# One encoder layer on one core: head groups moved in single transfers, high parts on the lower rows

## The chip, the cores and the metric

The kernel runs on one core of one Trainium2 chip. The number that counts is device time in microseconds (us) of one execution, start to end. Engines have the names of the profile: PE is the matrix engine (TensorE), PEld its weight loads, DVE is VectorE, ACT is ScalarE, POOL is GpSimd, SP is SyncE, which only issues transfers here. A transfer (DMA) issued by SP is carried out by 16 DMA engines that serve the core.

## The reference

One layer of a transformer encoder over x, 2048 tokens of 1024 floats, all in float32. Two groups of 8 query heads (head size 64, 2 key/value heads each) read one projection:

```
h    = rms_norm(x) ; qa, ka, va, qb, kb, vb = split(h @ w_in)
A:  q, k rms-normalised per head, 2-D rotary positions,
    softmax(q k^T / 8) v over all 2048 keys
B:  1-D rotary positions, keys with |i - j| <= 128 only,
    m = max(max(s), sink) ; e = exp(s - m)
    o = (e @ v) / (sum(e) + exp(sink - m))
y    = x + rms_norm([rms_norm(A), rms_norm(B)] @ w_out)
out  = y + rms_norm((silu(h2 @ w_gate) * (h2 @ w_up)) @ w_down),  h2 = rms_norm(y)
```

## The kernel before, in words

Every large product is done in three passes on PE: each operand is split into a high part in the reduced format (fp32r) and a low part that holds the rest, and high*high, high*low and low*high are added up. The two parts of a head group's queries lie under each other in one tile of 128 rows: the 64 rows of head size for the one, the other 64 for the other.

The program has four stretches in time. From 0 to about 455 us it projects: 16 tiles of 128 tokens, one after another (`proj`), while side work for earlier tiles runs between the projection's products: `heads` turns queries and keys of tile t-1 round and splits them, `bmax`, `battn`, `brec` and `bfin` (L1057 to L1150) do the windowed attention (group B) of tiles t-2 and t-3, and in the tiles with t from 4 to 11 `w_out_prep` (L1393) scales and splits one 128-row slice of w_out. From 455 to 500 us the last windowed tiles pass into the global attention (group A), which runs to about 1225 us with the output projection. The rest is the feed-forward part, which the change doesn't touch.

All work is recorded first. A list scheduler (`Plan.order`, L330) then writes the order of every engine, with fixed costs of its own: a transfer costs its bytes over 350 bytes per ns, after 1100 ns, SP is busy 450 ns per issue, and a reader can start 1000 ns (PE: 1350 ns) after its end. It knows no DMA engines. What it chooses is then issued engine by engine (L523, so that all rows of the profile stand at line 523). Engines work in that order: an instruction that waits holds up all that stand behind it on its engine. All transfers go through SP's one queue (`load`, L617).

The names that matter below, in the order in which a tile passes through them:

- `heads` (L1004): `HL` holds the split queries, rows by head pair: row half g belongs to head group g, the two columns of blocks to high and low. There is one buffer for HL, used first for group B and then for group A. Four transfers of 64x512 spread B's HL to `RB`, where group g has its high part on row half g; A's HL goes to DRAM as `QA` in one. `KA`, the split keys of A, goes to DRAM as `KD` in four transfers.
- `bmax` (L1057): two transfers put the 64 high rows of each group from RB into `R2B`; eight products with maxima on DVE give `mx`, which PE turns round and ACT writes as `mr`; mr goes into row 64 of R2B (the shift row), and two rows of the sink's exponential, `eh`, into rows 96 and 97 (`ES_ROW`).
- `battn`: products `mm<-R2B,K2B` add the shift; exponentials `pf`, split into `ph` and `pl`; sums in `o`. `den_row` (L1262) copies the row of sums into row 0 or 64 of `rb` and sends it to `cmp`, a 16x64 tile.
- `brec`: reciprocal of cmp, stored as `RDB`; `spread` (L1272) reads it back, one head group's row into each of 64 rows of `rb`, in two transfers. `bfin` multiplies `oT` by rb.
- The global attention does the last two steps with `cmpa`, `RDA` and `dena`, and `load_q` (L1215) fetches its queries R from QA, eight transfers of 64x512 a tile.
- `w_out_prep`: per 512 columns two loads of 64 rows, 256 rows apart, into `woraw`; ACT writes `wohi`, DVE `wolo`, and both go to DRAM as `WO`.

```
for h in range(2):                                                                  # w_out_prep, before
    self.load(raw[ROWS[h]], self.i["w_out"][r0 + 256 * h:r0 + 256 * h + HD, n * 512:(n + 1) * 512])
for g in range(2):                                                                  # spread, before
    src = scratch[8 * g:8 * g + 8].rearrange("(o c) x -> o (c x)", o=1)
    self.load(rb[ROWS[g]], src.broadcast_to([HD, 512]))
```

Of the kernel before, what the change touches and what calls it, by code (L numbers as in the profile page):

```python
# [50 lines left out]
EARLY = 4  # L51
EARLY_NS = 2000
KV_NS = 3500
ES_ROW = 96
B0 = 432
B_TAIL = 13
T0_BANKS = (("mm", "ow", "o1"), ("mm", "a1", "a2"))
# [468 lines left out]
class Layer:  # L526
    def __init__(self, ctx, tc, ins, out):
        self.tc, self.nc, self.plan = tc, tc.nc, None
        self.i = ins
        self.out = out  # L530
        nc = self.nc
        dram = ctx.enter_context(tc.tile_pool(name="dram", bufs=1, space=DRAM))
        def scratch(name, shape, n):
            return [self.wrap(dram.tile(shape, F32, name=f"{name}{i}"), shape) for i in range(n)]

        self.QA = scratch("QA", [P, 2, 512], NT)
        self.KD = scratch("KD", [P, 512], NT // 2)
        self.VD = scratch("VD", [P, 768], NT // 2)
        self.WO = scratch("WO", [P, 8, 512], 4)
        self.OB = scratch("OB", [P, 512], NT)  # L540
        self.SH = scratch("SH", [8, P], NT)
        self.MX = scratch("MX", [P, D], NT)
        self.RDA = scratch("RDA", [16, HD], NT)
        self.RDB = scratch("RDB", [16, HD], NT)
        self.X2 = scratch("X2", [P, D], NT)
        self.XA = [scratch(f"XA{c}_", [P, 2, 4, P], 4) for c in range(2)]
        self.XB = [scratch(f"XB{c}_", [P, 5, 4, P], 4) for c in range(2)]
        self.AC = [scratch(f"AC{c}_", [P, 7, CH], NFF // 2) for c in range(2)]

        cp = ctx.enter_context(tc.tile_pool(name="const", bufs=1))  # L550
        self.ident = cp.tile([P, P], F32, name="ident")
        make_identity(nc, self.ident)
        self.z1 = cp.tile([P, P], F32R, name="z1")
        nc.vector.memset(f32(self.z1)[:, 0:HD], 0.0)
        nc.vector.memset(f32(self.z1)[:, HD:P], 1.0)
        self.ones2 = cp.tile([P, 2], F32, name="ones2")
        self.warm = cp.tile([P, 2], F32, name="warm")
        nc.vector.memset(self.ones2, 1.0)
        self.mhalf = cp.tile([P, 16], F32, name="mhalf")
        nc.vector.memset(self.mhalf, -0.5)  # L560
        self.sink_b = cp.tile([P, 8], F32, name="sink_b")
        self.sink_c = cp.tile([8, 1], F32, name="sink_c")
        self.flag = cp.tile([1, 1], mybir.dt.int32, name="flag")


        self.down_s = cp.tile([P, 1], F32, name="down_s")
        self.up_s = cp.tile([P, 1], F32, name="up_s")
        self.gg = cp.tile([P, 8], F32, name="gg")
        self.gpre = cp.tile([P, NK], F32, name="gpre")
        self.gf = cp.tile([P, NK], F32, name="gf")  # L570
        for name, v in list(vars(self).items()):
            if hasattr(v, "shape") and not isinstance(v, View):
                setattr(self, name, self.wrap(v, v.shape))
# [234 lines left out]
    def b_consts(self):  # L808
# [21 lines left out]
            nc.gpsimd.memset(f32(self.va[r])[:, :, P:], 1.0)  # L830
        self.K1B, self.RB = {}, {}
        self.R2 = bp.tile([ES_ROW + 2, 2, 512], F32R, tag="R2B", bufs=1, name="R2B")
        nc.gpsimd.memset(f32(self.R2)[HD:ES_ROW + 2], 0.0)
        self.zs = bp.tile([ES_ROW + 2, P], F32R, tag="zs", bufs=1, name="zs")
        nc.gpsimd.memset(f32(self.zs), 0.0)
        nc.gpsimd.memset(f32(self.zs)[ES_ROW:ES_ROW + 2, HD:P], 1.0)

# [24 lines left out]
    def w_in_tiles(self, j):  # L864

        if j < 4:
            return [self.wk.tile([P, 512], F32R, tag=f"ks{3 * j + n}", bufs=1, name="w_in") for n in range(3)]
        w = (self.wk if j < 8 else self.wq).tile([P, 1536], F32R, tag=f"kv{j}", bufs=1, name="w_in")
        return [w[:, n * 512:(n + 1) * 512] for n in range(3)]

    def urgent(self, ns):
        if self.plan:
# [131 lines left out]
    def heads(self, t):  # L1004
# [14 lines left out]
        for s in ((t - 4) // 4, t // 4, (t + 4) // 4):  # L1019
            pos = t - (4 * s - 1)  # L1020
            if 0 <= s < NT // 4 and 0 <= pos < 6:
                if s not in self.K1B:
                    self.K1B[s] = bp.tile([P, 2, 6 * P], F32R, tag="K1B", bufs=2, name="K1B")
                dst.append(self.K1B[s][:, :, pos * P:(pos + 1) * P])
        for g in range(2):
            for h in range(2):
                for d in dst:
                    nc.scalar.activation(d[ROWS[h], g, :], tk[ROWS[g], 1, :], AF.Copy)
            for h in range(2):
                self.load(kd[ROWS[g if h == 0 else 1 - g], g, :], f32(KA)[ROWS[g], h, :])  # L1030
            nc.vector.tensor_tensor(k2b[0:HD, g, :], tk[ROWS[g], 1, :], f32(dst[0])[ROWS[g], g, :], op=ALU.subtract)
        yield 218
        for src, R in ((rb, RB), (ra, None)):
# [7 lines left out]
            if R is None:  # L1041
                self.load(self.QA[t], f32(HL))
            else:
                for g in range(2):
                    for h in range(2):
                        self.load(f32(R)[ROWS[g if h == 0 else 1 - g], g, :], f32(HL)[ROWS[g], h, :])
            yield 436
        self.RB[t] = RB

# [7 lines left out]
    def bmax(self, t):  # L1057
# [1 line left out]
        nc, bp, sm = self.nc, self.bp, self.sm  # L1059
        RB = self.RB[t]  # L1060
        R2 = self.R2
        for g in range(2):
            self.load(f32(R2)[0:HD, g, :], f32(RB)[ROWS[g], g, :])
        lo = 1 if t == 0 else 0
        hi = 2 if t == NT - 1 else 3
        n = (hi - lo) * P
# [119 lines left out]
    def shifts(self):  # L1186

        nc, sm = self.nc, self.sm
        for t in range(NT):
            RA = [self.kv.tile([P, 512], F32R, tag="pha", bufs=NPH, name="RAs") for g in range(2)]  # L1190
            for g in range(2):
                for h in range(2):
                    self.load(f32(RA[g])[ROWS[g if h == 0 else 1 - g]], self.QA[t][ROWS[g], h, :])
            mx = sm.tile([P, 8, 4], F32, tag="mx4", name="mx4")
            for h in range(8):
                g, p = h // 4, h % 4
# [18 lines left out]
    def load_q(self, t):  # L1215
        if t >= NT or t in self.qt:
            return
        R1 = self.kv.tile([P, 2, 512], F32R, tag="R1", name="R1")
        for g in range(2):
            for h in range(2):  # L1220
                self.load(f32(R1)[ROWS[g if h == 0 else 1 - g], g, :], self.QA[t][ROWS[g], h, :])
        self.qt[t] = R1
        for g in range(2):
            R2 = self.wk.tile([P, 512], F32R, tag=f"ks{8 + (2 * t + g) % 4}", bufs=1, name="R2")
            for h in range(2):
                self.load(f32(R2)[ROWS[1 - g if h == 0 else g]], self.QA[t][ROWS[g], h, :])
            self.qs[t, g] = R2

    def load_shift(self, t):
        self.sh_row[t] = self.kv.tile([1, 2, 512], F32R, tag="shr", bufs=1, name="shr")  # L1230
# [30 lines left out]

    def den_row(self, rb, src, cmp, g):  # L1262

        row = rb[HD * g:HD * g + 1]
        self.nc.scalar.activation(row, src[HD:HD + 1], AF.Copy)
        self.load(cmp[8 * g:8 * g + 8], row.rearrange("o (c x) -> o c x", x=HD))

    def recip(self, cmp, scratch):
        self.nc.vector.reciprocal(cmp, cmp)
        self.load(scratch, cmp)  # L1270

    def spread(self, rb, scratch):  # L1272
        for g in range(2):
            src = scratch[8 * g:8 * g + 8].rearrange("(o c) x -> o (c x)", o=1)
            self.load(rb[ROWS[g]], src.broadcast_to([HD, 512]))

    def normalize(self, o, den, j):
        cs = slice(j * P, (j + 1) * P)
# [114 lines left out]
    def w_out_prep(self, k):  # L1393

        nc, bp = self.nc, self.bp
        r0 = 512 * (k // 4) + HD * (k % 4)
        for n in range(2):
            raw = bp.tile([P, 512], F32, tag="pf", bufs=2, name="woraw")
            for h in range(2):
                self.load(raw[ROWS[h]], self.i["w_out"][r0 + 256 * h:r0 + 256 * h + HD, n * 512:(n + 1) * 512])  # L1400
            hi = bp.tile([P, 512], F32R, tag="ph", bufs=PB, name="wohi")
            lo = bp.tile([P, 512], F32R, tag="pl", bufs=PB, name="wolo")
            nc.scalar.activation(hi, raw, AF.Copy, scale=self.gg[:, k:k + 1])
# [429 lines left out]
```

## Time and profile before

| | us |
|---|---|
| median of 3 runs (2551.17 to 2563.43) | 2554.9 |
| the profiled execution | 2557.14 |
| its span on the core | 2555.3 |
| PE busy | 2462.4 (96%) |
| DVE busy | 1877.8 (73%) |
| POOL busy | 1473.4 (58%) |
| ACT busy | 1393.1 (55%) |
| SP's queue: share of the 16 DMA engines' span | 42.5% |

The span is the time from the first to the last instruction that the profiler saw; 1.84 us lie around it. Busy time of one engine overlaps that of the others, so the shares don't add up. The DMA share is a mean over 16 engines: it doesn't say how a single transfer is spread over them.

### The profile page before, as it was taken

Reading aid. Unit: us, or ns where it says so; the run is one execution under the profiler, and the core shown is the slowest. Engines: PE = TensorE matmul, PEld = TensorE weight load, DVE = VectorE, ACT = ScalarE, POOL = GpSimd, SP = SyncE. Lnnn points to the kernel's source line nnn. Section 1 sums busy time; section 2 is a strip of 40 time slices with the busy share of each in tenths; the row PEclk is TensorE's granted clock in tenths of the full one; section 3 lists DMA queues with packets and bytes.
Section 4 is the critical chain, followed back from the end, with each engine's and each line's share of the span. In section 5 each row is a group of like instructions: output and inputs, shape, how many; then the busy total and the mean of one; then the engine's idle time right before and its main releaser. Section 6 shows DMA issues by size and latency. Waiting matters only on the chain.

```text
span 2555.3 us, 34171 instructions
## 1 busy us (share of the span) xinstructions
PE 2462.4 (96%) x10604; PEld 1945.0 (76%) x10604; DVE 1877.8 (73%) x2864; ACT 1393.1 (55%) x2610; POOL 1473.4 (58%) x1175
## 2 busy tenths in 40 slices
PE   8999999899999999999899999999999999999997
PEld 6766677577877777777688888878888887888886
DVE  6777677789898988888877667796655556556755
ACT  5666566598888888878433333343332334433433
POOL 4333343379998889999365666755445443331333
PEclk9999999999999999999999999999999999999999
DMA  6555544443121313222544445563233227554664
GB/s 200 153 157 158 159 146 129 144 157 100 61 88 64 100 63 107 96 91 92 173 147 142 159 154 166 179 223 112 91 97 122 87 83 262 174 182 148 184 200 154
DMA packets 200896, 351.67 MB, mean 138 GB/s; under 512 B 26624, under 2 KB 82304, under 8 KB 200192
## 3 DMA queue, kind: packets, MB, share of 16 engines
q1 hardware_dynamic: 200704, 349.40, 42.5%
q8 instruction: 85, 1.39, 0.2%
q14 instruction: 107, 0.88, 0.1%
HBM read 229.85 MB, written 106.56 MB: 132 GB/s over the span
## 4 chain that ended last, share of the span: by engine, by line
PE 75%; DVE 7%; ACT 6%; DMA 5%; issue 4%; POOL 2%; SPq 1%; ACTq 0%; DVEq 0%; POOLq 0%
PE gu L523 31%; PE gv L523 18%; PE mm L523 6%; PE ow L523 6%; PE o L523 6%; PE a L523 4%; PE pp L523 3%; DVE pla L523 1%; DMA xn<-in_x_dram 1%; SPq L523 1%; ACT pha L523 1%; ACT mm L523 1%; POOL acc L523 1%; ACT nat L523 1%; DMA RB<-HL 1%
## 5 line engine op out<-in xcount | busy, mean ns | idle before, releaser
L523 POOL TENSOR_TENSOR acc<-acc,pha 128x512 f32<-128x512 f32 x408 | 561.3, 1386 | 48.9 <-ACT pha L523 22.5
L523 POOL TENSOR_TENSOR s<-wraw 128x512 f32<-128x512 f32 x88 | 124.3, 1425 | 304.4 <-DMA wraw<-in_w_up_dram 179.5
L523 PE MATMUL gu<-xl,wh 128*128 128x512 f32 x776 | 294.1, 396 | 0.0
L523 PE MATMUL gu<-xh,wl 128*128 128x512 f32 x776 | 288.1, 397 | 4.2 <-DVE wl L523 4.1
L523 PE MATMUL gu<-xh,wh 128*128 128x512 f32 x776 | 288.2, 397 | 1.8 <-ACT wh L523 1.8
L523 DVE TENSOR_TENSOR pla<-mm,pha 128x512 fp32r<-128x512 f32 x370 | 246.3, 682 | 34.4 <-ACT pha L523 24.0
L523 ACT ACTIVATE wh<-s 128x512 fp32r<-128x512 f32 x176 | 110.8, 630 | 281.5 <-PE gu L523 160.4
L523 PE MATMUL mm<-R,kt 128*128 128x512 f32 x740 | 251.0, 400 | 6.0 <-DVE pla L523 4.9
L523 PE MATMUL pp<-w_in,xh 128*128 128x512 f32 x720 | 239.2, 404 | 16.5 <-ACT w_in L523 10.9
L523 POOL TENSOR_TENSOR c<-c,c 128x512 f32<-128x512 f32 x132 | 203.4, 1557 | 77.5 <-DVE c L523 52.3
L523 DVE TENSOR_TENSOR al<-ar,ah 128x512 fp32r<-128x512 f32 x154 | 140.1, 913 | 146.9 <-ACT ah L523 131.7
L523 ACT ACTIVATE mm<-mm 128x512 f32<-128x512 f32 x370 | 214.6, 591 | 28.5 <-PE mm L523 26.1
L523 ACT ACTIVATE ah<-ar 128x512 fp32r<-128x512 f32 x154 | 97.0, 630 | 224.7 <-PE gu L523 137.2
L523 DVE TENSOR_TENSOR c<-gu,c 128x512 f32<-128x512 f32 x174 | 116.4, 686 | 115.8 <-PE gu L523 115.3
L523 DVE TENSOR_TENSOR wl<-s,wh 128x512 fp32r<-128x512 f32 x176 | 164.9, 942 | 20.9 <-ACT wh L523 11.5
L523 PE MATMUL gv<-xl,wh 128*128 128x512 f32 x456 | 175.1, 396 | 2.2 <-DVE xl L523 2.2
L523 PEld LDWEIGHTS gu<-xh,wl 128*128 128x128 f32 x776 | 146.1, 189 | 39.2 <-DVE wl L523 5.0
L523 ACT ACTIVATE wh<-wraw 128x512 fp32r<-128x512 f32 x132 | 83.0, 628 | 168.3 <-PE gu L523 97.6
L523 PEld LDWEIGHTS gu<-xh,wh 128*128 128x128 f32 x776 | 146.3, 189 | 36.9 <-ACT wh L523 2.7
L523 PEld LDWEIGHTS mm<-R,kt 128*128 128x128 f32 x740 | 134.7, 188 | 50.2 <-DVE pla L523 21.2
L523 PEld LDWEIGHTS pp<-w_in,xh 128*128 128x128 f32 x720 | 136.0, 191 | 48.5 <-ACT w_in L523 13.1
L523 PEld LDWEIGHTS gu<-xl,wh 128*128 128x128 f32 x776 | 146.4, 189 | 34.5
(257 smaller groups left out, 6522.0 us busy)
## 6 DMA issues: line engine op xcount, KB each, us to landing
AC<-c SPq DMA_DIRECT2D x154, 256.0 KB
ar<-AC SPq DMA_DIRECT2D x154, 256.0 KB
wdr<-in_w_down_dram SPq DMA_DIRECT2D x99, 256.0 KB
wraw<-in_w_gate_dram SPq DMA_DIRECT2D x20, 1024.0 KB
wraw<-in_w_up_dram SPq DMA_DIRECT2D x20, 1024.0 KB
R<-QA SPq DMA_DIRECT2D x128, 128.0 KB
st<-XB SPq DMA_DIRECT2D x40, 256.0 KB
xn<-in_x_dram SPq DMA_DIRECT2D x16, 512.0 KB
```

Source lines behind the costliest of these rows:

```text
L523: op.call(*[real(a) for a in op.args], **{k: real(v) for k, v in op.kw.items()})
```

## The change

Transfers that came in pairs or fours, one for each head group or for each part, become one for both, with the head group as a dimension of the transfer:

- RB is filled by way of DRAM: one store QB<-HL of 128x1024, then two loads RB<-QB of 64x2x512. High parts of both groups now lie on the lower rows.
- KD<-KA: two stores with both groups (2x64x128) for four of 64x128.
- R2B<-RB: one of 64x1024 for two of 64x512.
- cmp<-rb and cmpa<-dena: one transfer of rows 0 and 64 (16x1x64), after the second copy, for two of one row each.
- rb<-RDB and dena<-RDA: one for two; the source has the shape group x 64 copies x 512.
- woraw<-w_out: one for two; the source has the shape 2 x 64 x 512.
- R<-QA in the attention: four of 64x2x512 a tile for eight of 64x512, and tiles in pairs (`w_in_slot`) so that both groups' R2 lie beside each other.
- ES_ROW is 65: the sink rows lie next to the shift row, and the rows between need no zeros.

```diff
--- before.py
+++ after.py
@@ -51,7 +51,7 @@
 EARLY = 4
 EARLY_NS = 2000
 KV_NS = 3500
-ES_ROW = 96
+ES_ROW = HD + 1
 B0 = 432
 B_TAIL = 13
 T0_BANKS = (("mm", "ow", "o1"), ("mm", "a1", "a2"))
@@ -534,6 +534,7 @@
             return [self.wrap(dram.tile(shape, F32, name=f"{name}{i}"), shape) for i in range(n)]
 
         self.QA = scratch("QA", [P, 2, 512], NT)
+        self.QB = scratch("QB", [P, 2, 512], NT)
         self.KD = scratch("KD", [P, 512], NT // 2)
         self.VD = scratch("VD", [P, 768], NT // 2)
         self.WO = scratch("WO", [P, 8, 512], 4)
@@ -830,10 +831,10 @@
             nc.gpsimd.memset(f32(self.va[r])[:, :, P:], 1.0)
         self.K1B, self.RB = {}, {}
         self.R2 = bp.tile([ES_ROW + 2, 2, 512], F32R, tag="R2B", bufs=1, name="R2B")
-        nc.gpsimd.memset(f32(self.R2)[HD:ES_ROW + 2], 0.0)
         self.zs = bp.tile([ES_ROW + 2, P], F32R, tag="zs", bufs=1, name="zs")
         nc.gpsimd.memset(f32(self.zs), 0.0)
-        nc.gpsimd.memset(f32(self.zs)[ES_ROW:ES_ROW + 2, HD:P], 1.0)
+        nc.gpsimd.memset(f32(self.zs)[HD:ES_ROW + 2, HD:P], 1.0)
+        nc.gpsimd.memset(f32(self.zs)[HD:HD + 1, HD:P], 0.0)
 
 
 
@@ -864,9 +865,16 @@
     def w_in_tiles(self, j):
 
         if j < 4:
-            return [self.wk.tile([P, 512], F32R, tag=f"ks{3 * j + n}", bufs=1, name="w_in") for n in range(3)]
+            return [self.w_in_slot(3 * j + n) for n in range(3)]
         w = (self.wk if j < 8 else self.wq).tile([P, 1536], F32R, tag=f"kv{j}", bufs=1, name="w_in")
         return [w[:, n * 512:(n + 1) * 512] for n in range(3)]
+
+    def w_in_slot(self, i):
+        if i < 8:
+            return self.wk.tile([P, 512], F32R, tag=f"ks{i}", bufs=1, name="w_in")
+        if i % 2 == 0:
+            self.pair = self.wk.tile([P, 2, 512], F32R, tag=f"kq{(i - 8) // 2}", bufs=1, name="w_in")
+        return self.pair[:, i % 2, :]
 
     def urgent(self, ns):
         if self.plan:
@@ -1022,12 +1030,12 @@
                 if s not in self.K1B:
                     self.K1B[s] = bp.tile([P, 2, 6 * P], F32R, tag="K1B", bufs=2, name="K1B")
                 dst.append(self.K1B[s][:, :, pos * P:(pos + 1) * P])
+        for h in range(2):
+            self.load(kd[ROWS[h]].rearrange("r g c -> g r c"), f32(KA)[:, h, :])
         for g in range(2):
             for h in range(2):
                 for d in dst:
                     nc.scalar.activation(d[ROWS[h], g, :], tk[ROWS[g], 1, :], AF.Copy)
-            for h in range(2):
-                self.load(kd[ROWS[g if h == 0 else 1 - g], g, :], f32(KA)[ROWS[g], h, :])
             nc.vector.tensor_tensor(k2b[0:HD, g, :], tk[ROWS[g], 1, :], f32(dst[0])[ROWS[g], g, :], op=ALU.subtract)
         yield 218
         for src, R in ((rb, RB), (ra, None)):
@@ -1041,9 +1049,10 @@
             if R is None:
                 self.load(self.QA[t], f32(HL))
             else:
-                for g in range(2):
-                    for h in range(2):
-                        self.load(f32(R)[ROWS[g if h == 0 else 1 - g], g, :], f32(HL)[ROWS[g], h, :])
+                self.load(self.QB[t], f32(HL))
+                parts = self.QB[t].rearrange("(g r) h c -> h r g c", g=2)
+                for h in range(2):
+                    self.load(f32(R)[ROWS[h]], parts[h])
             yield 436
         self.RB[t] = RB
 
@@ -1059,8 +1068,7 @@
         nc, bp, sm = self.nc, self.bp, self.sm
         RB = self.RB[t]
         R2 = self.R2
-        for g in range(2):
-            self.load(f32(R2)[0:HD, g, :], f32(RB)[ROWS[g], g, :])
+        self.load(f32(R2)[0:HD], f32(RB)[0:HD])
         lo = 1 if t == 0 else 0
         hi = 2 if t == NT - 1 else 3
         n = (hi - lo) * P
@@ -1190,7 +1198,7 @@
             RA = [self.kv.tile([P, 512], F32R, tag="pha", bufs=NPH, name="RAs") for g in range(2)]
             for g in range(2):
                 for h in range(2):
-                    self.load(f32(RA[g])[ROWS[g if h == 0 else 1 - g]], self.QA[t][ROWS[g], h, :])
+                    self.load(f32(RA[g])[ROWS[h]], self.QA[t][ROWS[g], h, :])
             mx = sm.tile([P, 8, 4], F32, tag="mx4", name="mx4")
             for h in range(8):
                 g, p = h // 4, h % 4
@@ -1216,15 +1224,14 @@
         if t >= NT or t in self.qt:
             return
         R1 = self.kv.tile([P, 2, 512], F32R, tag="R1", name="R1")
-        for g in range(2):
+        R2 = self.wk.tile([P, 2, 512], F32R, tag=f"kq{t % 2}", bufs=1, name="R2")
+        parts = self.QA[t].rearrange("(g r) h c -> h r g c", g=2)
+        for R, a in ((R1, 0), (R2, 1)):
             for h in range(2):
-                self.load(f32(R1)[ROWS[g if h == 0 else 1 - g], g, :], self.QA[t][ROWS[g], h, :])
+                self.load(f32(R)[ROWS[h ^ a]], parts[h])
         self.qt[t] = R1
         for g in range(2):
-            R2 = self.wk.tile([P, 512], F32R, tag=f"ks{8 + (2 * t + g) % 4}", bufs=1, name="R2")
-            for h in range(2):
-                self.load(f32(R2)[ROWS[1 - g if h == 0 else g]], self.QA[t][ROWS[g], h, :])
-            self.qs[t, g] = R2
+            self.qs[t, g] = R2[:, g, :]
 
     def load_shift(self, t):
         self.sh_row[t] = self.kv.tile([1, 2, 512], F32R, tag="shr", bufs=1, name="shr")
@@ -1261,18 +1268,18 @@
 
     def den_row(self, rb, src, cmp, g):
 
-        row = rb[HD * g:HD * g + 1]
-        self.nc.scalar.activation(row, src[HD:HD + 1], AF.Copy)
-        self.load(cmp[8 * g:8 * g + 8], row.rearrange("o (c x) -> o c x", x=HD))
+        self.nc.scalar.activation(rb[HD * g:HD * g + 1], src[HD:HD + 1], AF.Copy)
+        if g == 1:
+            rows = rb.rearrange("(g r) (c x) -> g r c x", g=2, x=HD)[:, 0]
+            self.load(cmp, rows)
 
     def recip(self, cmp, scratch):
         self.nc.vector.reciprocal(cmp, cmp)
         self.load(scratch, cmp)
 
     def spread(self, rb, scratch):
-        for g in range(2):
-            src = scratch[8 * g:8 * g + 8].rearrange("(o c) x -> o (c x)", o=1)
-            self.load(rb[ROWS[g]], src.broadcast_to([HD, 512]))
+        src = scratch.rearrange("(g c) x -> g (c x)", g=2)
+        self.load(rb, src.unsqueeze(1).broadcast_to([2, HD, 512]))
 
     def normalize(self, o, den, j):
         cs = slice(j * P, (j + 1) * P)
@@ -1393,11 +1400,10 @@
     def w_out_prep(self, k):
 
         nc, bp = self.nc, self.bp
-        r0 = 512 * (k // 4) + HD * (k % 4)
         for n in range(2):
             raw = bp.tile([P, 512], F32, tag="pf", bufs=2, name="woraw")
-            for h in range(2):
-                self.load(raw[ROWS[h]], self.i["w_out"][r0 + 256 * h:r0 + 256 * h + HD, n * 512:(n + 1) * 512])
+            rows = self.i["w_out"].rearrange("(a r) c -> a r c", r=256)[2 * (k // 4):2 * (k // 4) + 2]
+            self.load(raw, rows[:, HD * (k % 4):HD * (k % 4) + HD, n * 512:(n + 1) * 512])
             hi = bp.tile([P, 512], F32R, tag="ph", bufs=PB, name="wohi")
             lo = bp.tile([P, 512], F32R, tag="pl", bufs=PB, name="wolo")
             nc.scalar.activation(hi, raw, AF.Copy, scale=self.gg[:, k:k + 1])
```

Since transfers have other costs in the planner, the order of all engines moves up to the feed-forward part. Three places follow, the first two in the first tile that prepares a slice of w_out.

SP's queue in that tile, before (destination, source, shape):

```order
L523 DMA woraw<-in_w_out_dram 64x512
L523 DMA RB<-HL 64x512 x4
L523 DMA KD_75<-KA 64x128
L523 DMA woraw<-in_w_out_dram 64x512
L523 DMA cmp<-rb 8x1x64
L523 DMA woraw<-in_w_out_dram 64x512 x2
L523 DMA KD_75<-KA 64x128
L523 DMA QA_61<-HL 128x1024
L523 DMA R2B<-RB 64x512
```

and in the changed kernel:

```order
L523 DMA KD_91<-KA 2x64x128
L523 DMA QB_78<-HL 128x1024
L523 DMA woraw<-in_w_out_dram 128x1x512
L523 DMA KD_91<-KA 2x64x128
L523 DMA RB<-QB_78 64x2x512
L523 DMA woraw<-in_w_out_dram 128x1x512
L523 DMA RB<-QB_78 64x2x512
L523 DMA R2B<-RB 64x1024
L523 DMA WO_105<-wohi 128x512
L523 DMA QA_62<-HL 128x1024
```

The loads of RB, of which the second stands behind both loads of w_out, have taken the place of four direct transfers between them.

ACT's queue in the same tile, before:

```order
L523 ACTIVATE xh<-x_t 128x512
L523 ACTIVATE HL<-mm 128x512
L523 ACTIVATE wohi<-woraw,gg 128x512
L523 ACTIVATE rb<-o_1414 1x512
L523 ACTIVATE oT<-o_1414 64x512
L523 ACTIVATE wohi<-woraw,gg 128x512
L523 ACTIVATE mr<-mm 8x128
L523 ACTIVATE es<-mr,sink_c 8x128
L523 ACTIVATE eh<-es 8x128
L523 ACTIVATE nat<-pp,rstd 128x512
```

and in the changed kernel:

```order
L523 ACTIVATE xh<-x_t 128x512
L523 ACTIVATE wohi<-woraw,gg 128x512
L523 ACTIVATE HL<-mm 128x512
L523 ACTIVATE rb<-o_1416 1x512
L523 ACTIVATE oT<-o_1416 64x512
L523 ACTIVATE wohi<-woraw,gg 128x512
L523 ACTIVATE mr<-mm 8x128
L523 ACTIVATE es<-mr,sink_c 8x128
L523 ACTIVATE eh<-es 8x128
L523 ACTIVATE nat<-pp,rstd 128x512
```

The first wohi now stands ahead of A's HL; mr and nat (which empties the projection's banks) stand behind the second wohi in both.

DVE's queue at the passage from the projection to the global attention, before, with the tiles' numbers (ISA is the masked maximum of a product and the reading of it, mx the row maxima):

```order
L523 ISA mm_4989,mx_4955<-mm_4989,band_278 128x384
L523 ISA mx_4955 128x1
L523 TENSOR_TENSOR HL_5005<-mm_4996,HL_5005 128x512
L523 ISA mm_5014,mx_4955<-mm_5014,band_278 128x384
L523 ISA mx_4955 128x1
L523 ISA mm_5017,mx_4955<-mm_5017,band_278 128x384
L523 ISA mx_4955 128x1
L523 TENSOR_TENSOR mx_4955<-mx_4955,sink_b_243 128x8
L523 TENSOR_TENSOR eh_5056<-es_5051,eh_5056 8x128
```

and in the changed kernel:

```order
L523 ISA mm_4913,mx_4878<-mm_4913,band_294 128x384
L523 ISA mx_4878 128x1
L523 ISA mm_4922,mx_4878<-mm_4922,band_294 128x384
L523 ISA mx_4878 128x1
L523 TENSOR_TENSOR mx_4878<-mx_4878,sink_b_259 128x8
L523 TENSOR_TENSOR HL_4935<-mm_4927,HL_4935 128x512
L523 TENSOR_TENSOR eh_4954<-es_4950,eh_4954 8x128
L523 RECIPROCAL cmp_4919<-cmp_4919 16x64
```

The low part of HL stood ahead of the last two maxima and now stands behind mx.

## Rows read from the trace of the kernel before

**Rows 1.** Busy time by stretch (start:end, length, engines, clock, DMA share, GB/s).

```profile
core 0: us, PE busy (x) PEld busy (x) DVE busy (x) ACT busy (x) POOL busy (x), PEclk, DMA share, GB/s
75.00:455.00 380.00, 358.85 (x1572) 272.04 (x1570) 275.76 (x602) 232.46 (x491) 142.30 (x161) 1.00 0.51 153
...
500.00:1225.00 725.00, 704.95 (x3012) 546.88 (x3012) 637.44 (x970) 597.99 (x1118) 646.07 (x502) 1.00 0.27 91
```

**Rows 2.** The page's line on packets and the queue's own.

```profile
DMA packets 200896, 351.67 MB, mean 138 GB/s; under 512 B 26624, under 2 KB 82304, under 8 KB 200192
...
q1 hardware_dynamic: 200704, 349.40, 42.5%
```

**Rows 3.** DMA issues, first and last of 60 groups and those named (KB each).

```profile
AC<-c SPq DMA_DIRECT2D x154, 256.0 KB
...
rb<-RDB SPq DMA_DIRECT2D x32, 128.0 KB
...
woraw<-in_w_out_dram SPq DMA_DIRECT2D x32, 128.0 KB
...
dena<-RDA SPq DMA_DIRECT2D x30, 128.0 KB
...
KD<-KA SPq DMA_DIRECT2D x64, 32.0 KB
...
R2B<-eh SPq DMA_DIRECT2D x32, 4.0 KB
cmp<-rb SPq DMA_DIRECT2D x32, 2.0 KB
...
cmpa<-dena SPq DMA_DIRECT2D x30, 2.0 KB
R2B<-mr SPq DMA_DIRECT2D x16, 4.0 KB
...
sink_c<-in_sink_b_dram SPq DMA_DIRECT2D x1, 0.0 KB
gf<-in_norm_ffn_pre_dram SPq DMA_DIRECT2D x1, 4.0 KB
```

**Rows 4.** The densest stretch of transfers in the attention, columns as in Rows 1.

```profile
550.00:575.00 25.00, 24.41 (x99) 17.64 (x99) 21.57 (x33) 24.20 (x48) 22.40 (x18) 1.00 0.82 326
```

**Rows 5.** Chain that ended last: start us, us, what.

```profile
182.49 2.81 DMA woraw<-in_w_out_dram
...
255.09 3.69 DMA rb<-RDB
```

**Rows 6.** Timeline of one w_out tile: start, us, engine, operation [idle before <-releaser].

```profile
241.02 1.19 SPq L523 DMA_DIRECT2D woraw<-in_w_out_dram  x2
...
246.44 0.72 ACT L523 ACTIVATE wohi<-woraw,gg 128x512 fp32r<-128x512 f32 x1 [1.18 <-DMA woraw<-in_w_out_dram]
...
248.42 0.27 ACT L523 ACTIVATE mr<-mm 8x128 fp32r<-8x128 f32 x1
...
252.23 0.47 PE L523 MATMUL mm<-R2B,K2B 65*128 65x512 f32 x1 [0.48 <-DMA R2B<-mr]
...
254.54 1.14 SPq L523 DMA_DIRECT2D rb<-RDB  x2
...
258.87 0.69 DVE L523 TENSOR_TENSOR oT<-oT,rb 128x512 f32<-128x512 f32 x1 [1.31 <-DMA rb<-RDB]
```

**Rows 7.** Waits of ACT, 75 to 455 us: us in total, times, longest.

```profile
ACT wohi L523 <- DMA woraw<-in_w_out_dram: 11.1, 10, 2.7
...
ACT HL L523 <- DMA RB<-HL: 2.9, 4, 1.7
```

**Rows 8.** Waits of DVE, 75 to 455 us, columns as in Rows 7.

```profile
DVE oT L523 <- DMA rb<-RDB: 14.6, 9, 3.2
```

**Rows 9.** Timeline of one attention tile's normalisation.

```profile
640.05 1.10 SPq L523 DMA_DIRECT2D dena<-RDA  x2
...
644.70 1.58 DVE L523 TENSOR_TENSOR oa<-oa,dena 128x512 f32<-128x512 f32 x1
```

**Rows 10.** Timeline of the passage to the attention.

```profile
457.47 0.27 PE L523 MATMUL mm<-ident,mx 128*8 128x128 f32 x1 [2.75 <-DVE mx L523]
```

## The prediction

> **What bounds the kernel now.** I read the busy time by stretch first, then the page's lines on packets and the queue's own, the list of DMA issues, the waits of ACT and DVE, and last the chain and the timeline where a changed transfer stands. The stretches show PE as the bound wherever the change is: 358.85 of 380 us in the projection, 704.95 of 725 in the attention [rows 1]. So there are 21 and 20 us of PE's waiting to win, and any new wait that reaches PE adds to the time. A projected tile takes about 27 us (380 us for 14 tiles).
>
> The same rows show DMA engines busy for 0.51 and 0.27 of their time [rows 1]. That is a mean over 16. The question of this change is how one transfer is dealt out to the 16, and the packets answer it. The queue moved 200704 packets [rows 2], of which 26624 are under 512 B. By the sizes in the program, 3080 of these are data of 4 B (the gain vectors, sink_c), 128 of 32 B (sink_b), 512 of 128 B (G) and 1504 of 256 B (gains, G, cmp, cmpa, RDB, RDA). That leaves 21400, which I take for the small packets that report the end of a transfer, one from each DMA engine that had a part in it. The 60 groups of the list add up to 1393 issues [rows 3]. With 16 reports each there would be 22288, which is 888 too many, and 888 is 111 times 8. Exactly 111 transfers have an outermost dimension of 8: R2B<-eh 32, cmp<-rb 32, cmpa<-dena 30, R2B<-mr 16, sink_c 1 [rows 3]. So a transfer with 8 outermost is done by 8 engines, and those with 64 or 128 by 16.
>
> This is also what the Trainium skill says, in DMA: Bandwidth & Descriptors, section "Why a DMA increments its semaphore by 16 and not by 1": the number of engines is the largest up to 16 that divides the slowest dimension on both sides, and they are the lowest-numbered ones. The trace agrees at 8, 64 and 128; no row of before has an outermost dimension of 2.
>
> **What the change makes of this.** Six forms now have 2 outermost on one side: KD<-KA (destination group x 64 x 128), cmp<-rb and cmpa<-dena (source rows 0 and 64), rb<-RDB and dena<-RDA (source group x 64 copies x 512), woraw<-w_out (source 2 x 64 x 512). Carrying the count on from 8 to 2, each runs on two engines, and I take them to be always the same two. QB, RB<-QB, R2B<-RB and R<-QA have 64 or 128 outermost and stay on 16.
>
> The price of one engine: 349.40 MB in 42.5% of 2555.3 us is 21.84 MB per engine in 1086 us, 20.1 GB/s [rows 2]; in a dense stretch 326 GB/s at a share of 0.82 is 24.8 GB/s per engine [rows 4]. A load of 256 KB on two engines is 128 KB each, 5.3 us at the faster rate and 6.5 at the slower. On 16 it is 16 KB each, 0.7 us. A KD store (32 KB each) takes 1.3 to 1.6 us of those two.
>
> **Part by part, against the profiled 2557.14 us.**
>
> A. *w_out, 8 tiles.* Two loads now stand in SP's queue with QB, KD and RB between them. On the two engines the loads alone take 10.6 us, where they took 1.4. What waits: in the tile of the timeline the loads were issued from 241.02 on, the second wohi ran at 246.44 after a wait for its load, mr at 248.42, and PE's mm<-R2B,K2B at 252.23 after a wait for the transfer that carries mr [rows 6]. Each step there had no slack left. ACT works in order, and behind the second wohi stand mr, es, eh and nat; nat empties the projection's banks, so PE gets neither the window products nor the next banks. ACT already waited for these loads ten times, 11.1 us in all [rows 7]. I take 10 us per tile: the 10.6 less what the loads took, plus a little of KD's 2.6 to 3.2. The low bound is 2, from load alone: per tile the two engines carry 448 KB (256 w_out, 128 rb, 64 KD), 18.5 us at 24.8 GB/s, and their part of the rest, 153 GB/s [rows 1] over 16 for 27 us, 258 KB or 10.4 us, 29 us in a tile of 27. The high bound is 18, if RB, of which the second half now stands behind both loads in the queue, is late by the whole stack and hides none of it (two loads at 6.5, two KD at 1.6, and QB's share). 8 x 10 = 80; bounds 16 and 144.
>
> B. *rb, 14 tiles of the projection.* One load of 256 KB in the place of two on 16 engines. Its wait is on the chain with 3.69 us now [rows 5], and DVE waited for it 14.6 us in nine tiles [rows 8], 1.31 in the one of the timeline [rows 6]. It lands 4.6 us later (5.3 less 0.7) to 5.8. DVE is in order and has other work behind it: low parts of x, HL and p, which PE needs. DVE has 104 us of idle time in the stretch [rows 1], so not all of it reaches PE. I take 4 per tile, near to the whole, as DVE already waits there: 56. Bounds 1 and 5.5 a tile, 14 and 77.
>
> C. *dena, 15 tiles of the attention.* Here the load was issued at 640.05 and used at 644.70, and DVE didn't wait [rows 9]. 4.6 to 5.8 us more end a little after that point, so the multiply waits for some 1 to 4 us, in a stretch where DVE is busy for 637 of 725 us. I take 1 us per tile that reaches PE: 15; bounds 0 and 30.
>
> D. *KD and cmp elsewhere*: KD's readers come in the attention, long after, and cmp is small. 3 us at the passage, where KD stands next to the last tile's chain; bounds 0 and 10.
>
> E. *Gains.* The second HL needn't wait for four transfers of the first: ACT's wait of 2.9 us in four [rows 7]. At the passage, the low part of HL no longer stands ahead of the last maxima on DVE, for which PE waited 2.75 us [rows 10]. Together 5; bounds 0 and 10. R2B<-RB, R<-QA and the issues that SP saves are worth nothing by themselves: no wait of ACT or DVE shown here is for SP's issuing. The sink rows and the memset cost nothing: the product with zs has 67 rows where it had 98, with the same 512 columns.
>
> Sum: 80 + 56 + 15 + 3 - 5 = 149, so 2706 profiled. The median of the runs is 2.2 below the profiled execution: **2704**.
>
> The Trainium skill has a rule for the change as well: DMA: Bandwidth & Descriptors, "Rules for kernel authors", says that two transfers to disjoint halves of the partitions share the same 16 engines one after the other, and that one transfer of 128 partitions is to be used instead. By that alone only E is left. The same table says that an outermost dimension under 16 confines the whole transfer to as many engines, and names the leading broadcast. The packets count against the first rule here, since its halves are now an outermost dimension.
>
> **The rivals.**
>
> R1, *the transfers stay wide*. If a dimension of 2 is merged with the 64 behind it before it is dealt out, every one of the six runs on 16 engines, lands as now or one issue earlier, and only the gains stay: 2.9 and 2.75 us of E, and 0.57 us (half of 1.14 [rows 6]) in nine waits for rb [rows 8], 5: 2546 profiled, 2544 as a median, not slower than before. It decides where a load of rb takes under about 4 us. For it: both sides hold 128 rows. Against it: the rows in DRAM don't follow on each other (256 rows apart, or the same row 64 times), and the eights in the packets were not widened either. Chance 0.08.
>
> R2, *two engines, but hidden*. The loads of w_out are issued early enough for ACT to have other work, and DVE finds its own in the idle 104 us. Then what stays is load (A at 3 us a tile, 24) and B at its low bound (14): 2595 profiled, 2593. For it: these 21 us of PE idle are small, and most waits of DVE and ACT don't reach PE. Against it: no slack in the timeline's tile. Chance 0.20.
>
> R3, *the two engines fill up*. 29 us of load in a tile of 27 at the faster rate, 36 at the slower (22.8 and 12.8): then a queue builds, and each transfer with 16 parts ends with its parts there, RB, the row of mr, x. A goes to 18 (144), B to 5.5 (77), C to 2 (30): 2557 + 251 + 3 - 5 = 2806, 2804. For it: the sum. Against it: a slower tile lowers the load. Chance 0.17.
>
> **How the numbers follow.** The forecast has 0.55. Its own range is 2640 to 2770. The range goes down to R2's 2593 and up a little beyond R3: 2590 to 2810, which leaves out R1 and some tails. A measurement of this kernel can tell about 0.5% (12.8 us) from no change. R1 is just within that, so half of its chance is faster and half the same: faster 0.04, same 0.05, slower 0.91.
>
> **What would show it.** Right: rb<-RDB and dena<-RDA with 8 us or more in the chain or from issue to use, where 3.69 stood; ACT waiting for woraw 8 to 15 us in each of eight tiles, and PE's mm<-R2B for the row of mr behind that; the projection about 135 us longer, the attention 10 to 20, the feed-forward part unchanged; fewer end packets, by 14 per transfer with 2 outermost. Wrong: rb lands in 4 us (R1); woraw is late but PE isn't (R2); waits for RB, x or QB, on 16 engines, longer than those for woraw (R3). If the feed-forward part changes by more than 10 us, I have missed something.

## The result: slower, with the time in the projection and half as much in the attention

The changed kernel takes 2692.1 us (median of 4 runs, 2682.8 to 2697.9), the kernel before 2559.2 in the runs beside it, 132.9 us less. The ratio is 1.0527, with a 95% interval of 1.0498 to 1.0556. 2704 was forecast.

The busy time of the profiled execution by stretch (start:end, length, then as in [rows 1]); the first border is 75 us in both kernels, the others stand at the same events (7 us before the last product of the projection, 16 us after the first product of the attention, 5 us before the feed-forward part):

```profile
75.00:541.60 466.60, 381.73 (x1527) 287.36 (x1526) 267.32 (x582) 232.28 (x489) 146.54 (x160) 0.91 0.43 138
588.00:1353.50 765.50, 717.77 (x3018) 549.80 (x3017) 650.58 (x974) 600.11 (x1120) 639.65 (x502) 0.99 0.27 86
1353.50:2681.00 1327.50, 1301.74 (x5655) 1056.40 (x5653) 887.62 (x1123) 493.64 (x857) 632.61 (x441) 0.99 0.48 156
```

Against [rows 1] the projection grew from 380 to 466.6 us (+86.6) and the attention from 725 to 765.5 (+40.5). The span grew from 2555.3 to 2681.0, 125.7 us (this execution is the fastest of the four), so that the head, the passage and the feed-forward part together are unchanged to 1.4 us. Of the 86.6 us in the projection, 63.7 are more idle time of PE (84.9 us in place of 21.2), and 22.9 are more busy time; the clock column, 0.91 in place of 1.00, is taken up at the end. The share of the DMA engines fell in the projection, from 0.51 to 0.43: by that mean nothing is short.

The page's lines on packets and the queue (as [rows 2]) and, from the list of DMA issues, the six forms (as [rows 3]):

```profile
DMA packets 197577, 360.02 MB, mean 134 GB/s; under 512 B 22284, under 2 KB 77964, under 8 KB 196876
...
q1 hardware_dynamic: 197388, 357.77, 41.5%
```

```profile
rb<-RDB SPq DMA_DIRECT2D x16, 256.0 KB
woraw<-in_w_out_dram SPq DMA_DIRECT2D x16, 256.0 KB
dena<-RDA SPq DMA_DIRECT2D x15, 256.0 KB
...
KD<-KA SPq DMA_DIRECT2D x32, 64.0 KB
...
cmp<-rb SPq DMA_DIRECT2D x16, 4.0 KB
...
cmpa<-dena SPq DMA_DIRECT2D x15, 4.0 KB
```

The six forms make 110 issues. The kernel has 1187 in all (1393 less 206). If a transfer reports from as many engines as its outermost dimension says, at most 16, the reports are 1187 x 16, less 14 for each of the 110, less 8 for each of 49 that still have 8 outermost (R2B<-eh 32, R2B<-mr 16, sink_c 1): 17060. With the 5224 packets of data under 512 B, as before, that is 22284: the page's number exactly.

Where the wait is seen, in the timeline of one tile that prepares w_out, first what ACT and SP did, then DVE and PE (columns as in [rows 6]):

```profile
316.35 0.58 SPq L523 DMA_DIRECT2D woraw<-in_w_out_dram  x1
...
320.59 2.14 SPq L523 DMA_DIRECT2D woraw<-in_w_out_dram  x1
...
325.05 0.72 ACT L523 ACTIVATE wohi<-woraw,gg 128x512 fp32r<-128x512 f32 x1 [4.23 <-DMA woraw<-in_w_out_dram]
...
325.80 0.75 DVE L523 SCALAR_TENSOR_TENSOR wolo<-woraw,gg,wohi 128x512 fp32r<-128x512 f32 x1 [4.06 <-ACT wohi L523]
...
327.14 0.44 PE L523 MATMUL mm<-K1B,RB 128*128 128x384 f32 x1 [3.97 <-DVE mx L523]
...
333.29 0.72 ACT L523 ACTIVATE wohi<-woraw,gg 128x512 fp32r<-128x512 f32 x1 [5.17 <-DMA woraw<-in_w_out_dram]
...
334.05 0.75 DVE L523 SCALAR_TENSOR_TENSOR wolo<-woraw,gg,wohi 128x512 fp32r<-128x512 f32 x1 [3.95 <-ACT wohi L523]
...
334.93 0.38 PE L523 MATMUL mm<-ident,mx 128*8 128x128 f32 x1 [2.55 <-DVE mx L523]
335.34 0.27 ACT L523 ACTIVATE mr<-mm 8x128 fp32r<-8x128 f32 x1 [1.33 <-PE mm L523]
```

The wait passes from the transfer to ACT, from ACT to DVE, which stands in order at wolo, and from DVE to PE, whose next maxima stand behind wolo. PE lost 3.97 and 2.55 us there. The lists of waits, 75 to 541.6 us, ACT, DVE and PE (us in total, times, longest, as in [rows 7, 8]):

```profile
ACT wohi L523 <- DMA woraw<-in_w_out_dram: 89.1, 16, 7.6
```

```profile
DVE wolo L523 <- ACT wohi L523: 66.1, 14, 7.5
DVE oT L523 <- DMA rb<-RDB: 38.1, 12, 5.6
```

```profile
PE mm L523 <- DVE mx L523: 34.4, 10, 5.2
PE o L523 <- DVE pl L523: 14.7, 12, 4.5
PE mm L523 <- DVE HL L523: 13.9, 6, 5.8
PE pp L523 <- ACT nat L523: 13.0, 4, 4.9
...
PE mm L523 <- DMA R2B<-mr: 0.7, 1, 0.7
```

Before, 75 to 455 us, DVE and PE had waited at these places for:

```profile
DVE wolo L523 <- ACT wohi L523: 6.7, 5, 2.9
```

```profile
PE pp L523 <- ACT nat L523: 1.9, 2, 1.6
...
PE mm L523 <- DVE mx L523: 0.6, 1, 0.6
```

The wait for woraw rose from 11.1 to 89.1 us, that for rb from 14.6 to 38.1, DVE's at wolo from 6.7 to 66.1, and PE's for mx from 0.6 to 34.4. In the attention, the chain has six loads of dena of 6.87 to 8.71 us (one shown; start, us), and the timeline shows DVE waiting where it didn't [rows 9]:

```profile
923.27 7.57 DMA dena<-RDA
```

```profile
740.72 0.52 SPq L523 DMA_DIRECT2D dena<-RDA  x1
...
747.60 1.68 DVE L523 TENSOR_TENSOR oa<-oa,dena 128x512 f32<-128x512 f32 x1 [3.02 <-DMA dena<-RDA]
```

### The profile page after: what moved, and what is told of

Its sections match the earlier page's. It is cut to its first block, busy times and chain, and to the rows that moved or that the text cites. A ratio compares the mean times of both kernels' runs of the same rounds, so it can differ in the third digit from the quotient of the medians.

```text
span 2681.0 us, 33754 instructions
## 1 busy us (share of the span) xinstructions
PE 2500.8 (93%) x10604; PEld 1967.8 (73%) x10604; DVE 1888.4 (70%) x2864; ACT 1395.8 (52%) x2610; POOL 1465.9 (55%) x1175
## 2 busy tenths in 40 slices
DMA packets 197577, 360.02 MB, mean 134 GB/s; under 512 B 22284, under 2 KB 77964, under 8 KB 196876
## 4 chain that ended last, share of the span: by engine, by line
PE 56%; DVE 4%; DMA 3%; issue 2%; POOL 1%; ACT 1%; SPq 0%; DVEq 0%; ACTq 0%; POOLq 0%
PE gu L523 30%; PE gv L523 18%; PE ow L523 3%; PE mm L523 2%; PE o L523 2%; PE a L523 2%; DMA dena<-RDA 2%; DVE pla L523 1%; POOL acc L523 1%; DMA RDA<-cmpa 0%; DVE st L523 0%; DVE oh L523 0%; ACT pha L523 0%; DVE oa L523 0%; ACT mm L523 0%
## 5 line engine op out<-in xcount | busy, mean ns | idle before, releaser
L523 PE MATMUL pp<-w_in,xh 128*128 128x512 f32 x720 | 253.3, 428 | 23.8 <-ACT nat L523 13.0
L523 PE MATMUL mm<-R,kt 128*128 128x512 f32 x740 | 256.7, 406 | 18.1 <-DVE pla L523 14.9
L523 PEld LDWEIGHTS pp<-w_in,xh 128*128 128x128 f32 x720 | 146.5, 207 | 59.5 <-ACT nat L523 16.0
L523 PEld LDWEIGHTS mm<-R,kt 128*128 128x128 f32 x740 | 134.2, 189 | 65.6 <-DVE pla L523 35.8
L523 PE MATMUL ow<-wo,oh 128*128 128x512 f32 x488 | 170.6, 397 | 8.9 <-DVE ms L523 4.6
```

The source lines that it names most:

```text
L523: op.call(*[real(a) for a in op.args], **{k: real(v) for k, v in op.kw.items()})
```

## The experiments

Two theories were to be told apart. The first is the forecast's: a transfer with 2 outermost is carried by two DMA engines, and its bytes take eight times as long. The second: the width is nothing, and the order of the engines, the way of RB by DRAM, or waiting for both halves in one costs the time.

**The same order, dealt wide.** The planner ran as in the changed kernel; only when an instruction is issued, the 110 transfers go out as two, by head group, so every engine's order stays and 64 (cmp: 8) is outermost.

```diff
+ elif op.eng == "SP" and split(op.kw):          # one side has 2 outermost, name in SPLIT
+     for g in range(2):
+         op.call(**{k: part(real(v), g) for k, v in op.kw.items()})
```

> The changed kernel with the order of every engine as it is; only the 110 transfers that have 2 outermost (KD, cmp, cmpa, rb, dena, woraw) are issued as two, one for each head group, so that 64 (cmp: 8) is outermost. Theory (two DMA engines carry those transfers): 2530 to 2565 us, near the kernel before, since only the small gains of the rest stay; under 512 B the packets rise by 110 x 14 + 110 x 16 less 62 x 8. Rival (the order of the engines, or RB by way of DRAM, is what costs): 2660 to 2700.

Measured: 2566.6 us, ratio 1.0039 (1.0026 to 1.0052), 1.6 us above the range expected. The packets rose as counted, to one more than 25088, and the wait for woraw went to 6.3 us (page, and waits of ACT from 75 to 455):

```profile
DMA packets 200383, 360.04 MB, mean 141 GB/s; under 512 B 25089, under 2 KB 80769, under 8 KB 199681
```

```profile
ACT wohi L542 <- DMA woraw<-in_w_out_dram: 6.3, 7, 1.6
```

125.5 of the 132.9 us are gone with no engine's order changed. Against all runs of before (median 2556.3) 10 us stay; the order, QB and the rest of the change together can't be the cause of more than that, on balance.

**The same order, halved the other way.** As above, but each of the 110 is cut along its columns, so that both halves keep 2 outermost.

```diff
  def part(ap, g):
-     n = ap.shape[0]
-     return (ap[g:g + 1] if ap.shape[1] == 8 else ap[g]) if n == 2 else ap[n // 2 * g:n // 2 * (g + 1)]
+     n = ap.shape[-1]
+     return ap[:, n // 2 * g:n // 2 * (g + 1)] if len(ap.shape) == 2 else ap[:, :, n // 2 * g:n // 2 * (g + 1)]
```

> The changed kernel with its order; the same 110 transfers are issued as two each, but halved along the columns, so that 2 stays outermost on both halves. Theory (width counts, not number or size): 2680 to 2710 us, as the changed kernel or a little slower for 110 more issues on SP. Rival (one large transfer is late because its reader waits for both halves in one): as fast as the kernel with halves by head group, under 2600.

Measured: 2734.0 us, ratio 1.0679 (1.0649 to 1.0708). Two transfers in place of one didn't help, which speaks against the merging. It was 42 us slower than the changed kernel, which neither theory had foreseen, and so it isn't a clean test: the pieces are half as long (1 KB for the loads, 256 B for KD) and there are 110 issues more. Which of the two costs the 42 us was not taken apart. The narrow load in the kernel before, further down, tests width with nothing merged.

**One form at a time.** The first edit, with a shorter list in each of four kernels.

```diff
- SPLIT = ("woraw", "rb", "dena", "KD", "cmp", "cmpa")
+ SPLIT = ("woraw",)        # then ("dena",), ("rb",), ("KD", "cmp", "cmpa")
```

> The changed kernel with its order; only the loads of w_out (16 transfers) are issued as two of 64 outermost. Theory: the eight tiles that prepare w_out lose most of their 84 us: 2605 to 2635. Rival (in those tiles rb and the KD stores are what holds them): 2660 or more.

> The changed kernel with its order; only dena<-RDA (15 transfers, attention) is issued as two of 64 outermost. Theory: the 33 us that the attention lost come back, nothing else moves: 2655 to 2668. Rival (the attention lost through cmpa, the pairs of R tiles or its order): 2680 to 2695.

> The changed kernel with its order; only rb<-RDB (16 transfers) is issued as two of 64 outermost. Theory (B is a term of its own, partly hidden beside the late loads of w_out): 2645 to 2672 us, 20 to 45 less than the changed kernel. Rival (rb is hidden wholly behind w_out and the rest): 2680 to 2697.

> The changed kernel with its order; only KD<-KA, cmp<-rb and cmpa<-dena (63 transfers) are issued as two with 64 or 8 outermost. Theory: the KD stores occupy the two engines for 2.6 to 3.2 us per tile and stand ahead of the loads of w_out in the queue, so something comes back in the eight tiles: 2670 to 2688 us. Rival (small and off the chain): 2688 to 2697.

| dealt wide | us | back, of 2692.1 |
|---|---|---|
| woraw | 2620.8 | 71.3 |
| rb | 2656.3 | 35.8 |
| dena | 2676.3 | 15.8 |
| KD, cmp, cmpa | 2681.5 | 10.6 |
| all | 2566.6 | 125.5 |

Each is a median of 4 runs that lie 5 to 17 us apart, so the small rows are known to a few us only. The four add up to 133.5, near to all at once: each form has its own part, and little of it is shared. Three came out within what the theory said; dena gave back half of what was expected. In the changed kernel DVE waited 19.9 us for it, in eight times (DVE's waits, 633 to 1359 us):

```profile
DVE oa L523 <- DMA dena<-RDA: 19.9, 8, 3.9
```

With dena wide that wait is gone, and 15.8 us of the time. Of what the attention lost, 20 us are still there with all forms wide (745 us in place of 725); the kernels with another plan, below, bear on where they come from.

**The narrow load alone, in the kernel before.** Here nothing of the change is in. The loads of w_out read the same number of rows, in as many transfers, with 2, 4 or 8 outermost. They read other rows of w_out.

```diff
- self.load(raw[ROWS[h]], self.i["w_out"][r0 + 256 * h:r0 + 256 * h + HD, n * 512:(n + 1) * 512])
+ rows = self.i["w_out"].rearrange("(a r) c -> a r c", a=2)[:, 32 * ((2 * k + h) % 16):32 * ((2 * k + h) % 16) + 32]
+ self.load(raw[ROWS[h]], rows[:, :, n * 512:(n + 1) * 512])
```

> The kernel BEFORE with its own order and the same number, size and piece length of transfers; only the 32 loads of w_out read 2 groups of 32 rows, 512 rows apart, in place of 64 rows in a row, so that 2 is outermost (they read other rows of w_out, so the output isn't the reference's). Theory: the eight tiles slow down as in the changed kernel: 2615 to 2650 us. Rival (the order or merging made the loss): 2550 to 2570.

> The kernel before with its order and as many bytes, pieces and transfers; the 32 loads of w_out read 4 groups of 16 rows, 256 rows apart, so 4 is outermost (other rows of w_out, the output isn't the reference's). Theory (the time goes with the bytes that one engine gets): four loads of 128 KB take 5.3 us on four engines in place of 10.6 on two; most of that was slack or is: 2560 to 2585 us, between the kernel before and the one with 2 outermost (2611). Rival (any outermost dimension under 16, or rows far apart, costs the same): 2600 to 2620.

> As the kernel with 4 outermost, with 8 groups of 8 rows, 128 rows apart (the output isn't the reference's). Theory: 2.6 us per tile on eight engines, hidden: 2550 to 2568 us, as before. Rival: 2600 to 2620.

| outermost | us | ratio to before (95%) | ACT's wait for woraw, us |
|---|---|---|---|
| 64 (before) | 2558.4 | | 11.1 |
| 8 | 2560.9 | 1.0014 (1.0001 to 1.0026) | 17.6 |
| 4 | 2575.4 | 1.0073 (1.0058 to 1.0088) | 33.7 |
| 2 | 2610.8 | 1.0219 (1.0194 to 1.0244) | 68.0 |

The waits of ACT, of the kernels with 2 and with 4 outermost (75 to 500 us), and the page's packets of these two; 32 transfers with 14 and with 12 reports fewer are 26176 and 26240:

```profile
ACT wohi L523 <- DMA woraw<-in_w_out_dram: 68.0, 16, 6.1
```

```profile
ACT wohi L523 <- DMA woraw<-in_w_out_dram: 33.7, 14, 3.5
```

```profile
DMA packets 200448, 351.67 MB, mean 135 GB/s; under 512 B 26176, under 2 KB 81856, under 8 KB 199744
```

```profile
DMA packets 200512, 351.67 MB, mean 137 GB/s; under 512 B 26240, under 2 KB 81920, under 8 KB 199808
```

Both counts are exact; with 8 outermost the page has 26369, one more than the 26368 that eight reports fewer per transfer would leave. From 2 to 8 outermost the wait falls by about half with each doubling (68.0, 33.7, 17.6), as expected if the bytes of one engine set when a load lands; the last step, to 11.1, is smaller. The time falls faster than the wait; that short waits are hidden would explain it, but was not followed up. With 2 outermost the kernel came out 4 us under the range expected.

**The change without narrow transfers, planned.** The code of before for KD, cmp, cmpa, rb, dena and w_out; the rest of the change stays. Then, on top, R<-QA in eight loads and the R tiles as before, so that RB by way of QB, R2B<-RB in one, the rows of KD and the sink rows are left.

```diff
- self.load(raw, rows[:, HD * (k % 4):HD * (k % 4) + HD, n * 512:(n + 1) * 512])
+ for h in range(2):                                   # likewise rb, dena, cmp, cmpa, KD
+     self.load(raw[ROWS[h]], self.i["w_out"][r0 + 256 * h:r0 + 256 * h + HD, n * 512:(n + 1) * 512])
...
- self.load(f32(R)[ROWS[h ^ a]], parts[h])
+ self.load(f32(R1)[ROWS[h], g, :], self.QA[t][ROWS[g], h, :])    # the second kernel alone, R2 likewise
```

> The changed kernel with KD, cmp, cmpa, rb, dena and w_out in the code of before (two or four transfers, planned as such); RB by way of QB, R2B<-RB and R<-QA merged and the sink rows stay. Theory: no wait of the kind left, the planner sees the true number of transfers: 2545 to 2570 us, at most 0.5% from before. Rival (the wide kernel with the order of the changed one was slow in the attention for its order alone): under 2550.

> The planned kernel with wide transfers (2560 us), with R<-QA in eight loads of 64x512 and R tiles not in pairs, as before the change; RB by way of QB, R2B<-RB in one and the sink rows stay. Theory: the number of issues on SP is nowhere on the path, so 2548 to 2565 us, no different. Rival (fewer, larger R loads help or hurt the attention): 2540 or less, or 2570 and more.

Measured: 2559.7 us, ratio 1.0010 (0.9994 to 1.0026), and 2550.3 us, ratio 0.9975 (0.9963 to 0.9987). The second is the fastest kernel here, by 0.25%, which is real by its interval and small. The attention of the three kernels without narrow transfers (windows from event to event; the wide one with the changed order, the first and the second planned one; columns as in [rows 1]):

```profile
492.00:1237.00 745.00, 711.32 (x3025) 545.61 (x3025) 657.76 (x977) 601.06 (x1124) 644.55 (x503) 1.00 0.29 88
```

```profile
495.10:1227.40 732.30, 708.35 (x3016) 550.03 (x3015) 642.47 (x970) 597.06 (x1118) 640.48 (x502) 0.99 0.29 90
```

```profile
490.60:1216.00 725.40, 704.07 (x3010) 547.18 (x3009) 636.33 (x969) 597.58 (x1117) 641.65 (x501) 1.00 0.28 91
```

So half of the 40.5 us that the attention lost came without a narrow transfer. 13 of these 20 us go when the same work, with R tiles in pairs, gets another plan (732.3); the other 7 go with the eight loads of R, the tiles not in pairs and the plan made for them (725.4, the length of before), and these were not told apart. Each length is from one execution, and which instructions cost the time was not pursued.

## Why the prediction was right, and where its terms were off

The mechanism was the forecast's: six forms of transfer on two engines, and waits for them that reach PE. The total came out within 12 us, but where the time went did not: about 135 us more had been expected in the projection and 10 to 20 in the attention, and 86.6 and 40.5 were measured. In the attention the sum had no term for the 20 us that came without a narrow transfer. That these errors nearly cancel is luck. Of the other signs, ACT's wait for woraw (11.1 us a tile on the mean of eight), the packets and the unchanged feed-forward part came; PE's wait for the row of mr did not.

*The count of engines* was the step on which all hung, and it held beyond what was forecast: exact at 2 and at 4, to one packet at 8.

*A, w_out*: 80 forecast, 71.3 given back when its loads were wide again. The eight tiles can be read from mr, which ACT writes once a tile: 96.43 and 340.84 us in the trace of before, 90.51 and 418.86 after, the first and the last end of eight tiles. That is 30.6 and 41.0 us a tile, 10.5 more:

```profile
96.43 0.27 ACT L523 ACTIVATE mr<-mm 8x128 fp32r<-8x128 f32 x1
...
340.84 0.27 ACT L523 ACTIVATE mr<-mm 8x128 fp32r<-8x128 f32 x1 [0.48 <-PE mm L523]
```

```profile
90.51 0.27 ACT L523 ACTIVATE mr<-mm 8x128 fp32r<-8x128 f32 x1 [1.19 <-PE mm L523]
...
418.86 0.27 ACT L523 ACTIVATE mr<-mm 8x128 fp32r<-8x128 f32 x1 [1.23 <-PE mm L523]
```

The size was right, the road was not. I let the wait reach PE by mr, R2B and nat, which stand behind wohi on ACT. nat cost PE 13.0 us, the row of mr 0.7. The larger part went by DVE, which stood 66.1 us at wolo, with the maxima of the window's scores behind it: 34.4 us of PE's waiting. In the kernel with w_out alone wide this wait is 0.4 us (75 to 541.6 us, as the next number). Another 13.9 us, 5.8 with w_out wide, went by the low part of HL: ACT's HL now stands behind the first wohi. I had looked up what is queued behind the waiting instruction on its own engine, and not what is behind the instruction on the next engine that waits for this one.

*B, rb*: 56 forecast, 35.8 given back. This is the term that was mis-sized: 35.8 us are 2.6 a tile over 14 tiles, not the 4 that I took. DVE's wait for rb was 38.1 us, and 3.4 with rb alone wide (75 to 541.6 us), so about as much as DVE waited came back, and what was too large is the wait itself. A reason that fits: in the eight w_out tiles rb and w_out are late in the same tile, and while DVE waits for ACT it doesn't wait for rb. With w_out alone wide the wait for rb is longer (the second line, 75 to 500 us):

```profile
DVE oT L542 <- DMA rb<-RDB: 3.4, 2, 2.4
```

```profile
DVE oT L542 <- DMA rb<-RDB: 47.2, 13, 6.2
```

*C, dena*: 15 forecast, 15.8 given back. *D, KD and cmp*: 3 forecast, 10.6 given back, a little over the bound of 10. The KD stores stand between the loads of w_out, and with KD and cmp wide ACT's wait for woraw is 82.1 us in place of 89.1. That fits transfers on the same two engines; which engines a transfer had, no row shows.

*E, the gains*: 5 forecast. The rest of the change is worth 6 us or so (0.25%) in the plan without pairs and nothing in the one with them, and it cost 10 in the plan of the changed kernel. Some gain came early: the row of mr at 90.51, in front of the first w_out tile, is 5.9 us ahead of that at 96.43; which part of the change gave it was not taken apart. What order a planner writes when its costs change wasn't in the sum at all, and it has about the size of these gains. At the passage PE's wait of 2.75 us for mx [rows 10] did go, and PE started the same product without one:

```profile
543.64 0.27 PE L523 MATMUL mm<-ident,mx 128*8 128x128 f32 x1
```

The sum, 149 forecast against 133 by the medians, is near also because A and B, 29 us too large together, stand against D and the order's 10 us, which were not seen. Of the rivals, R1 is out by the packets and by the wide kernel. Of R2's cover there was some, for rb. R3's queue showed on SP, told below, but the waits that were its sign stayed small: ACT waited 10.5 us for x and 9.6 for QB (75 to 541.6 us), against 89.1 for woraw.

## What to carry to other kernels

Two transfers made one are no gain if the pair becomes the outermost dimension: look at the slowest dimension on both sides, and keep it large, or leave them two (for the loads of w_out, against 64 outermost, 8 cost 0.14%, 4 0.7% and 2 2.2%). The count of small packets in a profile tells how many engines a transfer had, and a mean DMA share that falls while waits for transfers grow can be a sign that few engines carry the load. When a wait is priced, follow it through each engine in order: what stands behind the instruction that waits, and then what stands behind the instruction that waits for that one.

## What the runs showed that was not expected

SP itself was held up. Issuing a load of w_out took 0.5 to 0.6 us before, in all 32; in the changed kernel five of 16 took 1.3 to 4.0 us, one of them in the timeline above (320.59, 2.14 us), and of 32 loads of RB from QB three took 2.2 to 3.9 us, where 0.6 is usual. With the same order and wide transfers no issue of w_out took over 0.7 us, and none with KD and cmp alone wide, or in the kernel before with w_out alone narrow. So narrow loads of w_out by themselves, of 128 KB each, didn't hold SP up; the narrow stores of KD or of cmp have a part in it. All that stands behind such an issue in SP's one queue leaves later, whatever its width. What this cost was not taken apart.

TensorE's granted clock in the projection was 0.91 on the mean, where it was 1.00, in units of the upper level, 2.4 GHz: PE stood waiting more often, and the clock fell with it. The same 10604 products took 2500.8 us of busy time after and 2462.4 before, so up to 38 of the 126 us may be a price of the lower clock, for which my sum had no term. In the kernel with all forms wide it was 2466.5. No run here separates the clock from the waits.
